# A hybrid decoder layer: x and first weights interleaved, three column tiles on each quarter of x, later bias table, swapped attention outputs

## The chip, the cores and the metric

The kernel runs on one core of a Trainium2 chip. Its time is the device time of one execution in microseconds (us); before the change the median of three runs is 1372.5 us (1372.31 to 1373.0). Lower is better. The engines are TensorE (PE: matmuls, with PEld its weight loads), VectorE (DVE), ScalarE (ACT), GpSimd (POOL) and SyncE (SP, which here only issues DMAs).

## The reference

One layer of a causal decoder trunk for 256 tokens of 2048 features, all in fp32. Three sub-layers follow each other, each normalised before and after and added to the residual stream:

- a token mixer: `z = rmsnorm(x) @ w_in`, whose columns feed 12 heads of dilated window attention (64 wide, with a relative-position bias from a 32-row table), 512 channels of chunked spatial gating, and 12 heads of RWKV-7 (a recurrent state with data-dependent decay); their outputs go through `w_out`;
- cross-attention, 4 heads over 256 memory tokens;
- a gated MLP with 5632 hidden features and a causal convolution of width 3 (its taps) on the up-projection.

The attention part, cut to what matters here (one of three window patterns):

```python
scores = einsum(q, k) * dh ** -0.5
scores = where(valid, scores + bias, NEG_INF)
p = exp(scores - max(scores))
o = einsum(p, v) / sum(p)
```

The kernel merges the three patterns into one: the bias of a distance has the logarithm of the number of patterns that hold it added, and impossible distances get -1e30. The 12 head outputs together are then normalised (rmsnorm over 768 columns).

## The kernel before

**Products in split precision.** Each weight tile is loaded in pieces of 512 KB (`raw_load`, L217, on SP's queue, four buffers), and `split` (L227) makes two parts of it: a high part by a rounding copy on ACT (L233) and a low part, the rest, by a subtraction on DVE (L235); three buffers each. Activations have high and low parts too. A product then is three matmuls: high x high (L265), high x low (L267), low x high (L270), into a PSUM tile `mm`. `wstat` (L254) keeps weights stationary and streams 256 tokens; `xstat` (L291) keeps activations stationary and streams 512 columns (L306, L308, L312). A unit of 1024 weight elements per partition is split and used at once.

**Opening.** The pool `sp` takes x in eight tiles (two token halves of four column quarters), issued on SP (L416), with the first low-rank weights behind the first quarter. A table of gains, `grow` (64 rows, in two loads from ACT's queue, L433 and L434), is transposed on TensorE into `gpar` (L448, L449). `transposed` (L362) transposes x, two 128-column blocks at a time (L371), scales by the gain and splits into hT (ACT L357, DVE L358). `row_factors` (L384) squares and sums x on ACT (L391), and a power on POOL (L396) gives the row factor; `over_rows` (L399) spreads it (L403). Then come small parameters (`prow`, nine loads on SP, L486, transposed at L491), the bias table (`tab`, `oneh`, `lnc`: one small matmul, L510, an addition, L511, a store `toep` to DRAM, L513) and the convolution taps (`crow`, four transposes, L522, into `cw`).

**Main products and lanes.** The mixer's main stream of products runs over column tiles in a written order: the low-rank columns (128), three key tiles, three receptance and three value tiles of RWKV (256 columns each, L977), the gate's low-rank columns, attention's values, then q, k pairs and the gating columns (L1217 to L1224), then `w_out`. Beside it run lanes: generators for decays, keys, the triangular inverse, values, state, and later attention and gating (both only after the state is done). `Lanes` (L120) keeps its own clock, a planner's estimate: after each unit of main products it moves on by 2.6 us per eight blocks, and a lane that yielded a number of us is continued when that has passed; what a lane then puts on TensorE is placed behind the last main product. `L.drain` (L162) runs lanes until a condition holds. Then a scheduler of the language orders each engine's instructions by priority and its own estimate of when they are ready; `issue_after` pins an order on one engine only, and `high_priority` lifts instructions forward. Engines take their instructions in that fixed order.

**Parts of the lanes.** `decays` (L608) loads two small weights into one buffer `wa` from ACT's queue (L612, L613), multiplies them with the low-rank activations `zl` (L621), and takes sigmoids (L626) and later exponentials (L641, L642). `keys` (L661) squares (L669), sums (L674), takes a power on POOL (L680), spreads it (L682) and transposes it (L692).

**Attention.** `b12` (L1021) reads the stored table `toep` back from DRAM as 128 shifted rows for 12 heads, 1.5 MB. For each of three groups of four heads, two heads at a time: scores (L1038), addition of the bias and maxima on DVE (L1043 to L1047), exponentials on ACT with their sums (L1049, L1051), three transposes of the weights per head (L1059), and the outputs with the weights stationary and the values (64 columns) moving (L1066, L1068, L1070): tokens lie on the partitions. The result is divided by the sums (L1076), squared and summed (L1080); at the end it is scaled by the row factor (L1090), transposed (L1097) and split with a gain.

## Time and profile before

| | before |
|---|---|
| median of 3 runs | 1372.5 us |
| profiled execution, its own time | 1375.61 us |
| its span | 1373.9 us |
| mean granted TensorE clock | 0.993 |
| TensorE busy | 1337.0 us (97%) |
| VectorE / ScalarE / GpSimd busy | 869.4 / 715.7 / 149.6 us |

The profile is of one execution, recorded by the hardware; its span leaves out a little at either end. Rows of instruction groups give line, engine, operation, output <- inputs, shape, count, then busy time and the mean duration of one in ns, then the idle time of the engine before them and what ended it. A matmul's end is modelled, so that its duration is longer than its place in the stream: what one costs in a row of equals is the distance between starts, or the time per instruction in the chain of waits. fp32 matmuls count as two instructions each, those of split parts as one. In rows in order of time the first number is the start in us from the span's start, the second the time until the last of the group has ended; what stands in brackets is idle time of the engine before it and what ended that. Rows of waits give total us, times, and the longest.

### The profile page before, as it was taken

The page shows a single profiled execution, that of the slowest core. Times are in us where ns is not written, and L with a number is a line of the kernel's source. Part 1 is how long each engine was busy: PE and PEld are TensorE (multiplying, and loading weights), DVE is VectorE, ACT ScalarE, POOL GpSimd, SP SyncE. Part 2 cuts the span into 40 slices and gives each one's busy share as a digit, 9 for nine tenths or more (in the row PEclk, how much of TensorE's full clock was granted, in tenths as well). Part 3 has the DMA queues.
Part 4 walks back from the last instruction along what each step waited for, and adds up shares of the span by engine and source line. Part 5 has one row for each costly group of instructions (what it writes and reads, how often), then busy time and mean ns, then how long its engine had stood idle before and what let it go on. Part 6 is the DMA issues. An engine that isn't in the chain of part 4 may idle for free.

```text
span 1373.9 us, 20692 instructions
## 1 busy us (share of the span) xinstructions
PE 1337.0 (97%) x8036; PEld 1175.1 (86%) x8036; DVE 869.4 (63%) x1277; ACT 715.7 (52%) x1097; POOL 149.6 (11%) x185
## 2 busy tenths in 40 slices
PE   6899999999999999999999999999999999999997
PEld 6889989999987879878888888888888888888886
DVE  5579964456555766567767676767676674444444
ACT  5755363244446656456555555555555553434442
POOL 3011100120003110001111111111111120000001
PEclk9999999999999999999999999999999999999999
DMA  7545553145547755444655656666666666556663
GB/s 219 157 137 156 146 173 94 55 148 149 147 142 258 255 181 166 157 148 132 190 185 184 185 186 189 188 188 184 184 186 187 188 218 194 193 195 191 195 196 128
DMA packets 189840, 238.80 MB, mean 174 GB/s; under 512 B 7920, under 2 KB 144013, under 8 KB 189741
## 3 DMA queue, kind: packets, MB, share of 16 engines
q1 hardware_dynamic: 185802, 225.76, 53.1%
q0 software_dynamic: 3376, 11.29, 2.5%
q8 instruction: 63, 1.03, 0.3%
q10 hardware_dynamic: 563, 0.43, 0.1%
q14 instruction: 36, 0.29, 0.1%
HBM read 235.33 MB, written 2.12 MB: 173 GB/s over the span
## 4 chain that ended last, share of the span: by engine, by line
PE 91%; issue 3%; DVE 2%; DMA 1%; ACT 1%; POOL 1%; ACTq 0%; DVEq 0%; POOLq 0%
PE mm L284 24%; PE mm L286 12%; PE mm L306 10%; PE mm L308 10%; PE mm L312 10%; PE mm L265 6%; PE mm L270 5%; PE mm L267 5%; PE auxq L657 1%; DMA wa<-in_rwkv_w_up_dram 1%; DVE lo L235 1%; PE auxq L774 1%; PE auxp L774 1%; DMA raw<-in_w_in_dram 0%; ACT hi L233 0%
## 5 line engine op out<-in xcount | busy, mean ns | idle before, releaser
L235 DVE TENSOR_TENSOR lo<-raw,hi 128x1024 fp32r<-128x1024 f32 x422 | 517.5, 1227 | 392.9 <-ACT hi L233 391.6
L233 ACT CAST hi<-raw 128x1024 fp32r<-128x1024 f32 x422 | 442.9, 1050 | 468.0 <-PE mm L308 171.6
L284 PE MATMUL mm<-h,hi 128*128 128x512 f32 x1376 | 486.3, 399 | 0.0
L286 PE MATMUL mm<-h,lo 128*128 128x256 f32 x1376 | 386.5, 281 | 0.0
L284 PEld LDWEIGHTS mm<-h,hi 128*128 128x128 f32 x1376 | 258.6, 188 | 64.4
L286 PEld LDWEIGHTS mm<-h,lo 128*128 128x128 f32 x1376 | 260.0, 189 | 0.0
L265 PE MATMUL mm<-h,hi 128*128 128x256 f32 x624 | 162.6, 293 | 2.0 <-ACT h L357 2.0
L267 PE MATMUL mm<-h,hi 128*128 128x256 f32 x624 | 160.2, 288 | 0.7 <-DVE h L358 0.7
L308 PE MATMUL mm<-hi,hid 128*128 128x512 f32 x352 | 136.9, 389 | 0.0
L306 PE MATMUL mm<-hi,hid 128*128 128x512 f32 x352 | 136.9, 389 | 0.0
L265 PEld LDWEIGHTS mm<-h,hi 128*128 128x128 f32 x624 | 120.8, 195 | 4.3 <-ACT h L357 2.2
L267 PEld LDWEIGHTS mm<-h,hi 128*128 128x128 f32 x624 | 120.6, 194 | 1.7 <-DVE h L358 1.0
L1419 POOL TENSOR_TENSOR z<-z,rrow 128x256 f32<-128x256 f32 x86 | 70.7, 822 | 427.5 <-DVE z L1418 427.5
L312 PE MATMUL mm<-lo,hid 128*128 128x512 f32 x352 | 108.4, 389 | 0.0
L270 PE MATMUL mm<-h,lo 128*128 128x256 f32 x624 | 102.5, 286 | 0.0
L270 PEld LDWEIGHTS mm<-h,lo 128*128 128x128 f32 x624 | 87.2, 193 | 1.3 <-issue 1.0
L306 PE MATMUL mm<-hi,h 128*128 128x512 f32 (+1 forms) x208 | 79.1, 385 | 1.4 <-ACT hi L233 1.4
L312 PEld LDWEIGHTS mm<-lo,hid 128*128 128x128 f32 x352 | 66.1, 188 | 13.8
L308 PEld LDWEIGHTS mm<-hi,hid 128*128 128x128 f32 x352 | 66.1, 188 | 13.7
L306 PEld LDWEIGHTS mm<-hi,hid 128*128 128x128 f32 x352 | 66.0, 188 | 13.7
L308 PE MATMUL mm<-hi,h 128*128 128x512 f32 (+1 forms) x208 | 77.0, 375 | 0.0
L312 PE MATMUL mm<-lo,h 128*128 128x512 f32 (+1 forms) x208 | 59.8, 375 | 0.2 <-DVE lo L235 0.2
(336 smaller groups left out, 1520.5 us busy)
## 6 DMA issues: line engine op xcount, KB each, us to landing
raw<-in_ffn_w_up_dram SPq DMA_DIRECT2D x176, 512.0 KB, 3.6
raw<-in_w_in_dram SPq DMA_DIRECT2D x94, 512.0 KB, 4.3
raw<-in_ffn_w_down_dram SPq DMA_DIRECT2D x88, 512.0 KB, 4.6
raw<-in_w_out_dram SPq DMA_DIRECT2D x32, 512.0 KB, 5.0
raw<-in_mem_wkv_dram SPq DMA_DIRECT2D x16, 512.0 KB, 4.1
raw<-in_mem_wq_dram SPq DMA_DIRECT2D x8, 512.0 KB, 3.8
raw<-in_mem_wo_dram SPq DMA_DIRECT2D x8, 512.0 KB, 3.7
x<-in_x_dram SPq DMA_DIRECT2D x8, 256.0 KB, 7.4
```

The lines of the kernel that those rows point to most:

```text
L233: nc.scalar.copy(hv, rv)
L235: nc.vector.tensor_tensor(lv, rv, hv.bitcast(F32), op=ALU.subtract)
L265: nc.tensor.matmul(o, lhsT=hv[:, k, cs], rhs=X.h(k0 + k), start=(k0 + k == 0), stop=False)
L267: nc.tensor.matmul(o, lhsT=hv[:, k, cs], rhs=X.l(k0 + k), start=False, stop=False)
L270: L.last = nc.tensor.matmul(o, lhsT=lv[:, k, cs], rhs=X.h(k0 + k), start=False, stop=(k0 + k == nk - 1))
L284: nc.tensor.matmul(view(ps[t], z=2, t=S), lhsT=hv[:, k, cs], rhs=X.hl[k0 + k], start=(k0 + k == 0), stop=False)
L286: L.last = nc.tensor.matmul(ps[t][:, S:], lhsT=lv[:, k, cs], rhs=X.h(k0 + k), start=False, stop=(k0 + k == KT - 1))
L306: nc.tensor.matmul(o, lhsT=X.h(kk)[:, ts_], rhs=hv[:, k, :], start=(first and k0 + k == 0), stop=False)
L308: nc.tensor.matmul(o, lhsT=X.l(kk)[:, ts_], rhs=hv[:, k, :], start=False, stop=False)
L312: L.last = nc.tensor.matmul(o, lhsT=X.h(kk)[:, ts_], rhs=lv[:, k, :], start=False, stop=(last and k0 + k == nk - 1))
L774: nc.tensor.matmul(pv[:, n, c0:], lhsT=BN[:, g * 4 + n, :], rhs=G[g][:, n, c0:], start=True, stop=True)
L1419: nc.gpsimd.tensor_tensor(z, z, x2row, op=ALU.mult)
```

## The change

- **Opening.** SP issues x by quarters, with the low-rank weights (for quarters 0 and 2) and a quarter of the first key tiles' weights between them. Per quarter, `prepare` transposes and splits x and splits the weights, and three column tiles (low-rank, and two of the first key tile) take their products from it; the order on SP, ACT, DVE and TensorE is pinned by `queued`. The square sums of a quarter follow its splits on ACT. The first two `wstat` calls are gone.
- **Small loads.** `grow` has 48 rows; the memory gain's 16 rows (`grow2`), the nine parameter loads and the six decay weights (now three buffers, all loaded ahead) are issued from POOL.
- **Bias table and taps** move from the opening into the attention lane, with their loads on POOL and buffers of attention.
- **Lanes.** `keys` yields 5.5 in place of 3.5; the decays' exponentials are pinned behind the last sigmoid on ACT.
- **Attention.** The weights are divided by their sums before the transposes; the outputs have the values (64 columns) stationary and 256 or 128 tokens moving, so that they come out transposed, two heads on the two halves of the partitions. Squares are added over heads on POOL, summed over partitions by a small matmul, the row factor is spread by another, and the last transposes are gone.
- **Sizes.** Small tiles have 8 columns in place of 16; `v` and `oc` have rows of 544 in place of 516; two unused fillers are added.

```diff
+        cp.tile([P, 64], F32, name="fill")
...
-            return mk(cp, tag, bufs, (P, 16))[:, :n]
+            return mk(cp, tag, bufs, (P, 8))[:, :n]
...
+        def queued(*engines):
+            with_ = ExitStack()
+            for e in engines:
+                if e in last:
+                    with_.enter_context(tc.issue_after(last[e].ins))
+            return with_
...
+            nc.scalar.dma_start(grow, gains[0:6:2].rearrange("g (k p) -> g k p", p=P))
+            xt = [[], []]
+            raws = {}
+            for c in range(4):
+                with queued("SP"):
+                    load_row(xt, x2d, c, lambda: mk(sp, "x", 8), nc.sync)
+                if c % 2 == 0:
+                    with queued("SP"):
+                        raws["LO", c] = raw_load(w_in, 4 * c, 8, COL_LO, P, 0)
+                with queued("SP"):
+                    raws["K", c] = raw_load(w_in, 4 * c, 4, COL_CK, 2 * P, 0)
...
+            def prepare(c):
+
+                nonlocal lo_w, k_w
+                with queued("ACT", "DVE", "PE"):
+                    for _ in transposed(hT, xt, gcol(0), hbuf, js=(2 * c, 2 * c + 1), banks=(auxp, auxp)):
+                        pass
+                if c % 2 == 0:
+                    with queued("ACT", "DVE"):
+                        lo_w = split(raws["LO", c], 8, P, 0)
+                with queued("ACT", "DVE"):
+                    k_w = split(raws["K", c], 4, 2 * P, 0)
+
+            def first_products(c, o, w, k0, cs):
+                for k in range(4 * c, 4 * c + 4):
+                    for n, (wk, xk) in enumerate(((w[0], hT.h(k)), (w[0], hT.l(k)), (w[1], hT.h(k)))):
+                        L.last = last["PE"] = nc.tensor.matmul(o[:, :S], lhsT=wk[:, k - k0, cs], rhs=xk,
+                                                               start=(k == 0 and n == 0),
+                                                               stop=(k == KT - 1 and n == 2))
...
+            prepare(0)
+            for c in range(4):
+                kw = k_w
+                first_products(c, ps_lo, lo_w, 8 * (c // 2), slice(0, P))
+                first_products(c, ps_k[0], kw, 4 * c, slice(0, P))
+                if c < 3:
+                    prepare(c + 1)
+                    with queued("ACT"):
+                        square_sums(part, xt, c + 1, lambda: mk(sp, "tmp", 4))
+                first_products(c, ps_k[1], kw, 4 * c, slice(P, 2 * P))
+        rx = row_factors(xt, None, part)
...
-            nc.sync.dma_start(prow[r0:r0 + n, :], src.rearrange("(n p) -> n p", p=P))
+            nc.gpsimd.dma_start(prow[r0:r0 + n, :], src.rearrange("(n p) -> n p", p=P))
...
-            return mk(mp, "v", 3, (P, 516))
+            return mk(mp, "v", 3, (P, 544))[:, :516]
...
-            for i in range(3):
-                wa = mk(rp, "wa", 1, (P, 256))
-                nc.scalar.dma_start(wa[0:64, :], a["rwkv_w_up"][0][:, i * 256:(i + 1) * 256])
-                nc.scalar.dma_start(wa[64:128, :], a["rwkv_a_up"][0][:, i * 256:(i + 1) * 256])
+            was = [s1() for _ in range(3)]
+            for i, wa in enumerate(was):
+                nc.gpsimd.dma_start(wa[0:64, :], a["rwkv_w_up"][0][:, i * 256:(i + 1) * 256])
+                nc.gpsimd.dma_start(wa[64:128, :], a["rwkv_a_up"][0][:, i * 256:(i + 1) * 256])
...
+                with tc.issue_after(sig.ins):
+                    nc.scalar.activation(E2, E, AF.Exp, scale=KAPPA)
+                    nc.scalar.activation(E, E, AF.Exp, scale=-KAPPA)
...
-            yield 3.5
+            yield 5.5
...
+            rows, taps = et(), et()
+            nc.gpsimd.dma_start(rows[:REL_BUCKETS, :A_HEADS], a["rel_bias_table"])
+            nc.gpsimd.dma_start(rows[:REL_BUCKETS, P:P + 384], a["c_onehot"])
+            lnc = et()[:A_HEADS, :384]
+            nc.gpsimd.dma_start(lnc, a["c_lncount"])
...
+            yield 4.0
+            ps = auxp()
+            nc.tensor.matmul(ps[:A_HEADS, :384], lhsT=rows[:REL_BUCKETS, :A_HEADS], rhs=rows[:REL_BUCKETS, P:P + 384],
+                             start=True, stop=True)
+            nc.vector.tensor_tensor(lnc, ps[:A_HEADS, :384], lnc, op=ALU.add)
+            nc.gpsimd.dma_start(toep, lnc)
...
+                    nc.vector.reciprocal(rden, den)
+                    for e, sc in enumerate(scs):
+                        for b, w in ((0, slice(0, 128)), (1, slice(128, 384))):
+                            nc.vector.tensor_scalar(sc[:, w], sc[:, w], rden[:, 2 * e + b:2 * e + b + 1],
+                                                    None, op0=ALU.mult)
...
+                    for b, w in ((0, slice(0, S)), (1, slice(P, S))):
+                        for e in range(2):
+                            nc.tensor.matmul(po[64 * e:64 * e + 64, c0 + w.start:c0 + w.stop],
+                                             lhsT=vhead(b, 4 * j + e0 + e),
+                                             rhs=pts[e][:, b * S:b * S + w.stop - w.start],
+                                             start=(b == 0), stop=(b == 1))
...
+            for b in range(2):
+                nc.tensor.matmul(ps[:, b:b + 1], lhsT=asq[:, b * P:(b + 1) * P], rhs=cmask[:, 1, P - 1:P],
+                                 start=True, stop=True)
...
+                nc.tensor.matmul(ps[:, b * P:(b + 1) * P], lhsT=ars[:, b:b + 1].to_broadcast([P, P]), rhs=ident,
+                                 start=True, stop=True)
...
+            res.tile([P, 120], F32, name="fill2")
```

More of the change, by code (lines that the diff above doesn't have):

```diff
@@ L231, in split @@
             lv = lo[:, :nk * nco].rearrange("p (k c) -> p k c", k=nk)
-            with tc.high_priority(offset=AHEAD):
-                nc.scalar.copy(hv, rv)
-                with tc.issue_after(gcopy.ins):
-                    nc.vector.tensor_tensor(lv, rv, hv.bitcast(F32), op=ALU.subtract)
+            with tc.high_priority(offset=ahead):
+                last["ACT"] = nc.scalar.copy(hv, rv)
+                last["DVE"] = nc.vector.tensor_tensor(lv, rv, hv.bitcast(F32), op=ALU.subtract)
             return hv, lv
@@ new lines, in hybrid_block @@
+            nc.vector.memset(mhalf, -0.5)
+            nc.scalar.activation(small(1), mhalf[:, :1], AF.Square)
+            make_identity(nc, ident)
+            part = mk(cp, "rpart", 2, (P, 8))
+            ps_lo = auxq()
+            ps_k = [mmps(), mmps()]
+            lo_w = k_w = None
+            def prepare(c):
[8 more added lines that the diff above has]
+                    k_w = split(raws["K", c], 4, 2 * P, 0)
@@ new lines, in hybrid_block @@
+            ps = auxp()
+            nc.tensor.transpose(ps[:, :3 * KT], grow, ident[:3 * KT, :3 * KT])
+            last["DVE"] = nc.vector.tensor_copy(gpar[:, :3 * KT], ps[:, :3 * KT])
+            prepare(0)
+            for c in range(4):
+                kw = k_w
[6 more added lines that the diff above has]
+                first_products(c, ps_k[1], kw, 4 * c, slice(P, 2 * P))
@@ L981, in hybrid_block @@
                 g = new()
-                ps = wstat(w_in, col + i * 256, 2 * P, hT)
+                ps = [p[:, :S] for p in ps_k] if (key, i) == ("K", 0) else wstat(w_in, col + i * 256, 2 * P, hT)
                 gv = view(g, k=2, t=S)
```

198 lines of the change are left out of this document (82 added, 116 removed).

## The prediction

> **What bounds the kernel now.** I read the page first, then the engines by stretches of the opening, then what TensorE waited for, then the opening in order of time.
>
> ```profile
> PE 1337.0 (97%) x8036; PEld 1175.1 (86%) x8036; DVE 869.4 (63%) x1277; ACT 715.7 (52%) x1097; POOL 149.6 (11%) x185
> PE 91%; issue 3%; DVE 2%; DMA 1%; ACT 1%; POOL 1%; ACTq 0%; DVEq 0%; POOLq 0%
> ```
>
> TensorE is the bound: 97% busy, 91% of the chain that ends last. So a change can save only TensorE's idle time and TensorE's own work.
>
> ```profile
> core 0: us, PE busy (x) PEld busy (x) DVE busy (x) ACT busy (x) POOL busy (x), PEclk, DMA share, GB/s
> 0.00:10.00 10.00, 1.30 (x6) 1.21 (x7) 1.25 (x7) 4.23 (x8) 1.49 (x9) 1.00 0.69 204
> 10.00:20.00 10.00, 6.86 (x45) 6.22 (x44) 6.60 (x13) 7.37 (x18) 0.00 (x0) 1.00 0.95 283
> 20.00:30.00 10.00, 10.00 (x74) 10.00 (x73) 6.87 (x13) 6.95 (x16) 4.94 (x3) 0.83 0.57 164
> 30.00:40.00 10.00, 8.11 (x64) 7.29 (x63) 5.76 (x7) 2.09 (x2) 4.75 (x5) 1.00 0.84 256
> 300.00:420.00 120.00, 120.00 (x815) 107.66 (x814) 76.11 (x140) 60.73 (x114) 3.93 (x6) 1.00 0.50 148
> ```
>
> Of the 37 us in which TensorE is idle, 14 lie in the first 40. In the attention's stretch (300 to 420) it has none, so there only its own work counts.
>
> ```profile
> PE auxp L448 <- DMA grow<-in_mem_src_gain_dram: 8.7, 1, 8.7
> PE mm L265 <- ACT h L357: 2.0, 1, 2.0
> PE auxp L510 <- issue: 1.9, 1, 1.9
> PE auxp L692 <- ACT et L682: 1.6, 1, 1.6
> PE auxp L621 <- DMA wa<-in_rwkv_w_up_dram: 1.3, 1, 1.3
> ```
>
> These waits are what the change touches: the last part of the gain table, the opening's order, the bias table (L510), a decay weight (L621) and the keys' factor (L692).
>
> ```profile
> L265 PE MATMUL mm<-h,hi x48: 278/283/562, 12.3 to 39.6; 128*128 128x256 f32 x48
> L267 PE MATMUL mm<-h,hi x48: 278/283/519, 13.4 to 39.7; 128*128 128x256 f32 x48
> L270 PE MATMUL mm<-h,lo x48: 280/283/416, 20.2 to 40.2; 128*128 128x256 f32 x48
> ```
>
> This is my yardstick: the products of the low-rank tile and of the first key tiles are 144, and the last starts at 40.2 us. After it TensorE is nearly full, so whatever brings number 144 forward reaches the end.
>
> **The opening.** The same 5 MB (x 2, low-rank weights 1, key weights 2) are loaded by SP, now in quarters, and three column tiles use each quarter of x at once. By 20 us the rates above (204 and 283 GB/s over 10 us each) have moved 4.9 MB, so data is no longer late where the order asks for it at the pace worked out below.
>
> ```profile
> 6.75 0.63 ACT L391 ACTIVATE tmp<-x 128x512 f32<-128x512 f32 x1 [1.78 <-DMA x<-in_x_dram]
> 8.70 1.05 ACT L233 CAST hi<-raw 128x1024 fp32r<-128x1024 f32 x1 [1.22 <-DMA raw<-in_w_in_dram]
> 9.78 1.23 DVE L235 TENSOR_TENSOR lo<-raw,hi 128x1024 fp32r<-128x1024 f32 x1 [0.47 <-ACT hi L233]
> 11.89 0.84 ACT L357 ACTIVATE h<-auxp,gpar 128x256 fp32r<-128x256 f32 x2 [0.19 <-DVE h L358]
> 12.99 0.67 PE L371 MATMUL auxp<-ident,x 128*128 128x128 f32 x4
> 16.64 1.04 ACT L233 CAST hi<-raw 128x1024 fp32r<-128x1024 f32 x1 [2.44 <-DMA raw<-in_w_in_dram]
> 22.11 0.41 PE L267 MATMUL mm<-h,hi 128*128 128x256 f32 x1
> 22.32 0.41 PE L265 MATMUL mm<-h,hi 128*128 128x256 f32 x1
> ```
> ```profile
> 29.84 0.48 PE mm L270 x4
> 320.40 0.66 PE auxp L1059 x6
> ```
>
> A product takes 0.12 us, a 128-column transpose 0.11. Per quarter, counted from its first transpose: four transposes and the hop, 0.75 (as in the opening rows); four copies on ACT at 0.42, to 2.4; the key weights' high part 1.05, to 3.4; their low part on DVE 1.23, to 4.65. Meanwhile TensorE does the last quarter's twelve products and the low-rank tile's twelve (hidden); from 4.65 it does eleven key products, to 5.9, and only then come the next transposes. Quarter 2 also splits low-rank weights: ACT 1.05 more, DVE's two subtractions end at 3.45 + 2 x 1.23 = 5.9, next quarter at 7.2. Quarter 0: x is there at 6.75, with two square sums ahead on ACT; low-rank weights at 8.7; the key weights next in SP's queue some 1.7 later (512 KB at 300 GB/s), low part at 12.6, first key products done by 14 to 16, since the early products run at 0.21 (rows at 22). From 15: 5.9 + 7.2 + 5.9 + the last twelve 1.44 gives 35.5; I take 36. Ends: 33 (nothing cold, the splits overlap better) and 41 (cold throughout). The gain is 4.2, less TensorE work that was already done by 40.2 and now comes later, the bias table's:
>
> ```profile
> 37.60 0.80 PE L510 MATMUL auxp<-oneh,tab 32*12 32x384 f32 x2 [1.89 <-issue]
> 25.06 0.71 POOL L396 TENSOR_TENSOR rs<-small,mhalf 128x2 f32<-128x2 f32 x1 [22.93 <-DVE small L395]
> 39.87 0.55 POOL L513 DMA_DIRECT2D toep<-lnc  x1 [5.25 <-DVE lnc L511]
> ```
>
> **3.4 us** remain (ends 6.4 and -1.6). The L510 wait of 1.9 is inside this. The square sums move between the splits on ACT: 4.3 to 5.3 us of ACT work in quarters of 5.9 to 7.2, hidden. Sixteen small loads (parameters, mem gain, six decay weights) leave SP's and ACT's queues for POOL's: 16 x 0.55 = 9 us, in the 22.9 us in which POOL only waits. If they were issued behind the two big memsets after that power instead, they would come some 5 us late, and the decays with them.
>
> **Lanes.** The decay weights get three buffers: 1.3 us. The keys' transposes are issued 2 later in the planner's time, so the 1.6 us wait for L682 goes. The zl chain gets less cover, since its first products come straight behind the opening: I give back 0.7. Net **2.2 us** (ends 0.5 and 3.5). Sigmoids before exponentials save table loads,
>
> ```profile
> 47.42 1.28 ACT L626 ACT_TABLE_LOAD   x1
> ```
>
> two or three of them at 1.28; ACT is not the bound there, so nothing. The lanes start one key tile later against the main products (96 x 0.12 = 11.5 us less cover); attention's later groups wait for the main k tiles anyway, so nothing, at worst -3.
>
> **Attention.** Before, each pair of heads takes twelve 64-column instructions:
>
> ```profile
> 313.41 0.33 PE L1066 MATMUL auxq<-v,et 128*128 128x64 f32 x2
> ...
> 314.79 0.71 PE L1038 MATMUL auxp<-col,col 64*128 64x128 f32 x6
> ```
> ```profile
> 267.00 0.43 PE auxp L953 x2
> 304.59 0.86 PE auxp L1038 x8
> ```
>
> So 1.38 per pair, 8.3 for six pairs, and twelve transposes (L1097) at 0.11 = 1.3. Swapped, a pair has four instructions of 256 columns and four of 128, two heads on different halves of the output partitions, and no transposes at the end. One by one that is 4 x 0.215 + 4 x 0.11 = 1.30, 7.8 in all; L1038, the same eight sizes on two halves of the rows, takes 0.86, 5.2 in all. Added: four small matmuls, eight instructions at 0.11, 0.9. The saving is 0.9 to 3.5; I take **3.0**, nearer to L1038, since it is the same shape.
>
> [...]
>
> DVE gains 24 scalings and loses six and three broadcasts:
>
> ```profile
> L1090 DVE TENSOR_SCALAR ca<-ca,small 128x256 f32<-128x256 f32 x6 | 1.7, 348 | 0.8 <-POOL small L327 0.8
> ```
>
> At most 24 x 0.35 = 8 us more in 120 us where DVE is busy for 76: hidden; without that cover TensorE would wait for the low parts.
>
> The bias table now follows the state stage: loads, product, addition, a store to DRAM, the wide load.
>
> ```profile
> toep<-lnc POOLq DMA_DIRECT2D x1, 18.0 KB, 2.0
> ze<-toep POOLq DMA_DIRECT2D x1, 1536.0 KB, 9.7
> 300.81 0.64 POOL L1115 TENSOR_SCALAR_AFFINE_SELECT nat<-nat 128x512 f32<-128x512 f32 x1 [7.01 <-DMA nat<-in_sgu_w_dram]
> ```
>
> From the product to the landed bias: 0.8 + 0.55 + 2.0 + 9.7 = 13 us, against 3 of lane time before the scores; the first bias additions wait on DVE with splits queued behind them. The planner may hold these back, and splits run up to three tiles ahead, so I give back **1 us** (ends 0 and 13).
>
> **Aligned tiles and fillers.** The profile shows no addresses. Nearest are the products that read oc, one of the resized tiles, beside those that don't:
>
> ```profile
> L306 PE MATMUL mm<-hi,h 128*128 128x512 f32 x66 | 26.8, 406 | 0.0
> L306 PE MATMUL mm<-hi,oc 128*128 128x512 f32 x24 | 9.9, 411 | 0.0
> ```
>
> A difference of 5 ns on 72 products is 0.4 us either way; I take zero.
>
> **Sum.** 3.4 + 2.2 + 3.0 - 1.0 = 7.6 us. The profiled execution took 1375.6 (span 1373.9), 3.1 above the median of 1372.5; the saving is taken off the median: **1365 us**.
>
> **Rivals.**
> 1. The opening gives nothing: the copy, split and subtraction of each quarter keep number 144 near 40. For it: the 5.9 to 7.2 us a quarter are nearly all ACT and DVE, with TensorE behind them. Against: before, ACT's second split also waited 2.4 us for its weights (row at 16.64), with transposes' copies queued behind it. 1372.5 - 4.2 = 1368.3.
> 2. The clock. Before, TensorE was busy for 6.9 of the 10 us from 10 on, and the next 10 were granted 0.83, with products at 0.21. If the new order's pauses do this twice, some 36 more products and transposes on the path pay 0.1 each: 3.6 us, and 1369. [...]
> 3. Slower: the bias arrives late. The store waits in POOL's queue behind a mask that waits up to 7.0 us for its own load (row at 300.81), and the wide load after it; DVE stops at the addition. 13 + 7 - 3 of lane time = 17, less about 4 covered by tiles already split, is 13 us on TensorE: 1372.5 - 8.6 + 13 = 1377. It decides once the bias lands more than some 13 us after its scores. Against: the planner orders by its own reckoning of DMAs and may put main work ahead.
> 4. The order does nothing for time because planner shifts elsewhere cost as much: 1372.5.
>
> **How the numbers follow.** Chances: forecast 0.55 (its own range 1361 to 1369), rival 1 0.13, rival 2 0.10, rival 3 0.13, rival 4 0.09. A measurement of this kernel tells about 0.2%, 2.7 us. Faster: forecast, rival 1 and most of rival 2, 0.75; same: 0.12; slower: 0.13. The range leaves out rival 3 and the best corner of all terms (6.4 + 3.5 + 3.5 would be 1359): 1358 to 1373.
>
> **What will show it.** Number 144 starts at 33 to 38; the L510 and L621 waits are gone and L692's is under 0.5; quarters of 6 to 7 us in the opening; the swapped pairs take about 0.86 each; no gap on TensorE near the first score additions. Wrong if: PEclk falls in the second or third window; DVE waits for the ze load for more than 5 us; a swapped pair takes 1.3.

## The result and the profile after

The changed kernel takes 1379.7 us (median of 1376.7 to 1382.3), beside 1372.4 us for the kernel before on the same chip: ratio 1.0047, 95% interval 1.0029 to 1.0065. It is **slower**, by 6.5 us by the ratio and 7.3 by the medians, where I forecast 7.6 us less. Its profiled execution took 1379.5 us, close to its median.

The page of the changed kernel, busy time and the shares of the chain that ended last:

```profile
PE 1339.2 (97%) x8009; PEld 1169.8 (85%) x8009; DVE 876.3 (64%) x1302; ACT 708.0 (51%) x1083; POOL 166.3 (12%) x212
PE 89%; issue 4%; DVE 3%; ACT 2%; DMA 1%; POOL 1%; DVEq 0%; SPq 0%; POOLq 0%; ACTq 0%
```

TensorE is still the bound, with 27 instructions fewer but 2 us more of busy time, and the chain now runs through other engines for two points more. The stretches that I showed of before, now of the changed kernel (busy us and instructions of each engine, granted clock, DMA share, GB/s):

```profile
10.00:20.00 10.00, 9.20 (x54) 8.82 (x55) 4.38 (x7) 4.21 (x8) 3.53 (x7) 1.00 1.10 317
20.00:30.00 10.00, 7.80 (x62) 7.19 (x61) 5.43 (x7) 6.26 (x15) 0.00 (x0) 1.00 0.41 116
30.00:40.00 10.00, 9.58 (x78) 9.13 (x78) 7.41 (x12) 6.92 (x12) 4.72 (x3) 1.00 0.55 172
300.00:420.00 120.00, 117.43 (x776) 100.37 (x775) 80.74 (x174) 54.64 (x110) 13.38 (x17) 0.99 0.47 143
```

The opening is better filled. (Its clock of 1.00 from 10 to 20 us is measured only from 16.5 us on, where the records of the clock begin; until then products start 0.21 us apart, and 0.12 after.) The attention's stretch, which had no idle time at all before, has 2.6 us now and a clock below 1. What TensorE waited for in the changed kernel (total, times, longest):

```profile
PE auxp L493 <- DMA grow<-in_sandwich_gains_dram: 5.5, 1, 5.5
PE auxq L487 <- ACT hi L240: 3.9, 2, 2.5
...
PE auxp L1113 <- DVE et L1107: 2.0, 1, 2.0
PE auxp L651 <- ACT oc L656: 1.8, 1, 1.8
...
PE mm L318 <- DVE lo L241: 1.3, 1, 1.3
...
PE mm L312 <- ACT hi L240: 1.0, 1, 1.0
```

L493 and L487 are the opening. The other four are new or larger: the transposes of the probabilities (L1113) wait for DVE's scalings, the decays' second step (L651) for the sigmoids of the first, and the first tile of attention's values (L312, L318) for its splits. The waits at L510, L621 and L692 are gone.

The 6832 products of the main stream are the same in both kernels, so they can be counted off and compared. From the starts in the traces, the time (us) at which each part's last product begins:

| part | before | changed | table in a lane (e6) | lanes later (e9) | swap and table lane (e17) |
|---|---|---|---|---|---|
| low-rank and first key tile (144) | 40.2 | 37.3 | 36.4 | 41.8 | 38.9 |
| third key tile | 69.9 | 68.6 | 70.5 | 71.6 | 71.9 |
| second low-rank tile | 171.9 | 167.4 | 169.6 | 171.6 | 170.1 |
| first values tile (512 wide) | 195.0 | 192.8 | 195.3 | 198.5 | 193.1 |
| gate Bg | 327.5 | 318.1 | 319.7 | 325.3 | 322.3 |
| gate Bu | 411.0 | 414.3 | 407.7 | 414.6 | 406.2 |
| end of the span | 1373.9 | 1377.8 | 1370.4 | 1377.8 | 1368.2 |

From the gate Bu on all kernels run alike, within some 2 us. The changed kernel's lead of some 3 us at product 144 is 1.3 two tiles later; the 9.4 at Bg are not a saving, since lane work that lay ahead of Bg now lies behind it; by Bu the lane work is done in both and the changed kernel is some 3 us behind. (Before's profiled execution was 3 us over its median, so the median says 7.) The loss is made between product 144 and Bu. What of it lies behind Bg is best seen against e6, whose lane work lies in the same places: from Bg to Bu the changed kernel takes 96.2 us, e6 88.0. Of these 8.2 us TensorE's idle time is 2.2 (e6 has none), the half clock shown below costs 1.7 by estimate (half of its 3.4 us), and the table's product and the taps, which e6 has elsewhere, take about 1; some 3 us, in which TensorE is busy, are not accounted for. The same holds from product 144 to Bu against before: 377.0 us beside 370.8, with 8.2 us idle beside 5.5.

The chain that ended last, in the changed kernel (start, us, step):

```profile
319.87 0.76 PE auxp L1060 x2
...
320.65 0.56 DVE et L1062
...
321.49 2.96 DMA toep<-et
...
325.02 9.86 DMA ze<-toep
...
334.90 0.29 DVE et L1091
...
340.14 0.30 DVE et L1107
...
340.49 0.33 PE auxp L1113
```

From the table's product to the landed bias it is 15 us. The first scores were issued at 324.3; their additions begin at 334.9, the scalings at 340.1, and TensorE stops before the first transpose. What followed, in windows of the changed kernel of 3.4 us, the step in which the records of the clock change (the columns as above):

```profile
337.30:340.70 3.40, 1.35 (x12) 1.15 (x10) 3.37 (x8) 3.15 (x8) 0.00 (x0) 1.00 0.14 14
340.70:344.10 3.40, 3.40 (x19) 2.92 (x18) 2.70 (x5) 0.00 (x0) 0.00 (x0) 0.50 0.88 292
```

TensorE was busy for 1.35 of 3.4 us, and the next 3.4 us ran at half clock. The clock isn't what sets the two kernels apart, though: ahead of Bu the profiled execution of before has two such half-clock windows (at 19.9 and 262.3 us), the changed one only this. Over all executions the mean granted clock is 0.9935 in the four of the changed kernel and 0.9933 in the 17 of before in group 1.

### The profile page after: what moved, and what is told of

The parts are those of the page before. It is cut to its first block, busy times and chain, and to the rows that moved or that the text cites. A ratio compares the mean times of both kernels' runs of the same rounds, so it can differ in the third digit from the quotient of the medians.

```text
span 1377.8 us, 20669 instructions
## 1 busy us (share of the span) xinstructions
PE 1339.2 (97%) x8009; PEld 1169.8 (85%) x8009; DVE 876.3 (64%) x1302; ACT 708.0 (51%) x1083; POOL 166.3 (12%) x212
## 4 chain that ended last, share of the span: by engine, by line
PE 89%; issue 4%; DVE 3%; ACT 2%; DMA 1%; POOL 1%; DVEq 0%; SPq 0%; POOLq 0%; ACTq 0%
PE mm L290 23%; PE mm L292 12%; PE mm L312 10%; PE mm L314 10%; PE mm L318 10%; PE mm L271 5%; PE mm L276 5%; PE mm L273 5%; DVE lo L241 1%; PE mm L487 1%; PE auxq L688 1%; DMA ze<-toep 1%; ACT hi L240 1%; PE auxp L805 1%; PE auxq L805 1%
## 5 line engine op out<-in xcount | busy, mean ns | idle before, releaser
L241 DVE TENSOR_TENSOR lo<-raw,hi 128x1024 fp32r<-128x1024 f32 x422 | 516.8, 1226 | 388.7 <-ACT hi L240 386.8
L292 PE MATMUL mm<-h,lo 128*128 128x256 f32 x1376 | 386.5, 281 | 0.0
L290 PEld LDWEIGHTS mm<-h,hi 128*128 128x128 f32 x1376 | 258.6, 188 | 64.4
L292 PEld LDWEIGHTS mm<-h,lo 128*128 128x128 f32 x1376 | 260.0, 189 | 0.0
L271 PE MATMUL mm<-h,hi 128*128 128x256 f32 x576 | 148.2, 291 | 0.0
L273 PE MATMUL mm<-h,hi 128*128 128x256 f32 x576 | 146.7, 286 | 1.1 <-DVE h L364 1.1
L312 PE MATMUL mm<-hi,hid 128*128 128x512 f32 x352 | 136.9, 389 | 0.0
L273 PEld LDWEIGHTS mm<-h,hi 128*128 128x128 f32 x576 | 111.2, 193 | 2.5 <-DVE h L364 1.3
L271 PEld LDWEIGHTS mm<-h,hi 128*128 128x128 f32 x576 | 110.5, 193 | 2.9 <-issue 1.3
L318 PE MATMUL mm<-lo,hid 128*128 128x512 f32 x352 | 108.4, 389 | 0.0
L276 PE MATMUL mm<-h,lo 128*128 128x256 f32 x576 | 95.8, 286 | 0.0
L276 PEld LDWEIGHTS mm<-h,lo 128*128 128x128 f32 x576 | 81.0, 193 | 0.4 <-issue 0.3
L312 PE MATMUL mm<-hi,h 128*128 128x512 f32 (+1 forms) x208 | 79.2, 386 | 1.0 <-ACT hi L240 1.0
L318 PEld LDWEIGHTS mm<-lo,hid 128*128 128x128 f32 x352 | 66.1, 188 | 13.8
L312 PEld LDWEIGHTS mm<-hi,hid 128*128 128x128 f32 x352 | 66.1, 188 | 13.7
L318 PE MATMUL mm<-lo,h 128*128 128x512 f32 (+1 forms) x208 | 60.8, 378 | 1.4 <-DVE lo L241 1.3
```

The lines of the kernel that those rows point to most:

```text
L241: last["DVE"] = nc.vector.tensor_tensor(lv, rv, hv.bitcast(F32), op=ALU.subtract)
L271: nc.tensor.matmul(o, lhsT=hv[:, k, cs], rhs=X.h(k0 + k), start=(k0 + k == 0), stop=False)
L273: nc.tensor.matmul(o, lhsT=hv[:, k, cs], rhs=X.l(k0 + k), start=False, stop=False)
L276: L.last = nc.tensor.matmul(o, lhsT=lv[:, k, cs], rhs=X.h(k0 + k), start=False, stop=(k0 + k == nk - 1))
L290: nc.tensor.matmul(view(ps[t], z=2, t=S), lhsT=hv[:, k, cs], rhs=X.hl[k0 + k], start=(k0 + k == 0), stop=False)
L292: L.last = nc.tensor.matmul(ps[t][:, S:], lhsT=lv[:, k, cs], rhs=X.h(k0 + k), start=False, stop=(k0 + k == KT - 1))
```

## The experiments

The kernels below ran beside the kernel before on the same chip, whose median there is in the third column. All times in us.

| run | median | before | ratio | 95% interval |
|---|---|---|---|---|
| changed kernel | 1379.7 | 1372.4 | 1.0047 | 1.0029 to 1.0065 |
| e1 changed, table in the opening | 1376.0 | 1374.5 | 1.0007 | 0.9997 to 1.0018 |
| e2 changed, outputs not swapped | 1379.8 | 1374.5 | 1.0042 | 1.0030 to 1.0054 |
| e3 changed, old opening | 1381.1 | 1374.5 | 1.0051 | 1.0038 to 1.0064 |
| e4 changed, table in the opening, not swapped | 1379.0 | 1374.5 | 1.0043 | 1.0028 to 1.0057 |
| e5 before + new opening | 1381.2 | 1375.1 | 1.0050 | 1.0036 to 1.0065 |
| e6 changed, table in a lane of its own | 1373.2 | 1375.1 | 0.9990 | 0.9981 to 0.9999 |
| e7 changed, lanes' edits undone | 1384.0 | 1375.1 | 1.0072 | 1.0058 to 1.0086 |
| e8 changed, old tile sizes | 1380.7 | 1375.1 | 1.0041 | 1.0029 to 1.0053 |
| e9 before, lanes added one tile later | 1377.4 | 1374.2 | 1.0025 | 1.0013 to 1.0037 |
| e10 e6 + longer time between decays | 1375.8 | 1374.2 | 1.0009 | 0.9999 to 1.0019 |
| e11 e6 + time ahead of the inverse's copies | 1376.1 | 1374.2 | 1.0017 | 1.0007 to 1.0026 |
| e12 e6 + both | 1375.3 | 1374.2 | 1.0011 | 1.0000 to 1.0023 |
| e13 before + swap | 1372.1 | 1374.0 | 0.9989 | 0.9977 to 1.0001 |
| e14 before + lanes' edits | 1379.5 | 1374.0 | 1.0044 | 1.0029 to 1.0060 |
| e15 before + late table | 1379.1 | 1374.0 | 1.0033 | 1.0020 to 1.0047 |
| e16 before + swap and lanes' edits | 1374.8 | 1374.0 | 1.0009 | 0.9996 to 1.0021 |
| e17 before + swap and table lane | 1368.5 | 1374.9 | 0.9948 | 0.9929 to 0.9967 |
| e18 e17 + three decay weights | 1372.4 | 1374.9 | 0.9981 | 0.9968 to 0.9995 |

Differences between two rows carry both intervals, so they are good to some 2 to 2.5 us.

### Group 1: undo one part

e1 puts the table and the taps back into the opening:

```diff
+        nc.tensor.matmul(ps[:A_HEADS, :384], lhsT=tab, rhs=oneh, start=True, stop=True)
...
-            rows, taps = et(), et()
...
-            nc.vector.tensor_copy(cw, ps[:, :4 * NF].rearrange("p (j n) -> p j n", j=4))
             b12 = view(mk(rp, "ze", 1, (P, 3072)), h=A_HEADS, x=256)
```

> The changed kernel with the bias table and the taps loaded and multiplied in the opening again, as before the change; all else as changed. Theory A (the late bias is the loss): in the changed kernel's trace the first score addition waits 3.3 us for the wide load, the probabilities' transposes 2.05 us for their scalings, and the clock falls for 3.4 us behind that; 300 to 430 us holds 9.2 us more idle time on TensorE than before the change. Without the late bias most of it goes: 1379.7 - 7 + 2 (the opening gets the table's product and its loads back) = 1375, at most 1376.5, and no wait for the wide load. Theory B (the swapped outputs and their scalings are the loss): unchanged within 2 us, 1378 to 1381, and the transposes still wait. Theory C (the new opening bunches the lane work): also 1378 to 1381.

Ratio 1.0007: 5.5 us less than the changed kernel, as theory A has it. (The 9.2 us of added idle time from which I argued was misread: TensorE is busy for 126.4 of the 130 us from 300 on, and for all of them before, so it is 3.6.) But its opening pays: in its second key tile TensorE waits twice, first for `zl` and then for the sigmoids, the second time as in the changed kernel.

```profile
PE auxp L670 <- ACT oc L675: 1.8, 1, 1.8
PE auxp L670 <- ACT zl L1020: 1.3, 1, 1.3
```

e2 takes back the swapped outputs and keeps the late table:

```diff
-                                             lhsT=vhead(b, 4 * j + e0 + e),
-                                             rhs=pts[e][:, b * S:b * S + w.stop - w.start],
...
+                        nc.tensor.matmul(ov[:, 0, e, :], lhsT=pT[:, 0:P], rhs=vhead(0, h),
+                                         start=True, stop=True)
```

> The changed kernel with the attention outputs computed as before the change (probabilities stationary, the division after, twelve transposes at the end); the bias table stays late. Theory A (late bias): the first addition still waits some 3 us, and TensorE loses the 1.6 us that the swap saves in its own work: 1380 to 1382. Theory B (the 24 scalings on DVE ahead of the transposes, and the tiling changes, cost more than the swap saves): 1379.7 - 4 = 1376 or lower, and TensorE's wait for the transposes' input falls from 2.05 to under 1. Theory C (opening): 1379 to 1382.

No difference (1.0042). Theory B falls as far as it says that the scalings and the tilings cost more than the swap saves; theory A's loss of the swap's saving doesn't show either.

e3 is the kernel before with everything but the opening:

```diff
-            for c in range(4):
-                kw = k_w
-                first_products(c, ps_lo, lo_w, 8 * (c // 2), slice(0, P))
...
+        ps = wstat(w_in, COL_LO, P, hT)
```

> The kernel before with every part of the change but the opening: late bias, swapped outputs, aligned tiles, three decay weights, later keys. Theory A or B: the loss in the attention stays and the 3 us that the opening gained are gone: 1381 to 1384. Theory C (the opening's third column tile moves the lanes one key tile later and bunches their work): the loss goes with it, 1370 to 1374, and the groups of attention lie as before the change.

1.0051: beside the rest of the change, the opening is worth nothing that can be measured. Theory C, as the whole cause, falls.

e4 joins e1 and e2, so the attention is that of before:

```diff
-            rows, taps = et(), et()
...
-                                             lhsT=vhead(b, 4 * j + e0 + e),
```

> The changed kernel with both the bias table and the attention outputs as before the change: the new opening, the three decay weights, later keys and aligned tiles alone. By my sum of terms for these, 1372.4 - 3.4 - 2.2 + 1 (the table's product back in the opening) = 1368. Theory A or B: 1366 to 1371, since nothing of the changed attention is left. Theory C: 1377 to 1381, still slower than before the change.

1.0043, 1379.0 us, where theories A and B expected 1366 to 1371 and theory C, which fell in e3, 1377 to 1381. So a second loss stands in the opening and the lanes. And e4 against e1 prices the swap with the table early: 4.9 us.

### Group 2: the table's place, the opening alone, lanes, tiles

e5 is the kernel before with the new opening alone, the same edit as e3 the other way round:

```diff
+                first_products(c, ps_lo, lo_w, 8 * (c // 2), slice(0, P))
+                first_products(c, ps_k[0], kw, 4 * c, slice(0, P))
...
-        ps = wstat(w_in, COL_LO, P, hT)
```

> The kernel before with the new opening alone (loads interleaved, three column tiles on each quarter, small loads on POOL's queue); lanes, tile sizes, bias table and attention are those of before. Theory D (the low-rank tile is now done at the same time as the key tile, so the decays' chain behind it has less to hide under, and a halved clock follows the stall): what the opening wins by product 144 (1.3 to 3.8 us in the runs so far) is lost again before the second key tile is done, and the kernel is slower than before by 2 to 5 us, ratio 1.0015 to 1.0035. My first reckoning: faster by 3.4 us, ratio 0.9975. If the loss of 4.5 us in the run with both halves of the attention as before is due to the lanes' edits: ratio below 1.000.

1.0050: 6 to 7 us slower, over the 2 to 5 that theory D has. TensorE's waits between 40 and 210 us in e5:

```profile
PE mm L317 <- DVE lo L240: 3.2, 1, 3.2
PE auxp L668 <- DMA wa<-in_rwkv_w_up_dram: 2.4, 1, 2.4
PE auxp L668 <- ACT zl L1017: 1.3, 1, 1.3
```

The rows of the kernel before for the same three:

```profile
PE auxp L621 <- DMA wa<-in_rwkv_w_up_dram: 1.3, 1, 1.3
PE mm L306 <- ACT hi L233: 0.6, 1, 0.6
...
PE auxp L621 <- ACT zl L971: 0.3, 1, 0.3
```

e6 leaves the wide load behind the state stage and moves only the table's loads, product and store, and the taps, into a lane that starts with the others:

```diff
+        def tables():
+            w = mk(rp, "ze", 1, (P, 3072))
...
+            yield 16.0
+            ps = auxq()
+            nc.tensor.matmul(ps[:A_HEADS, :384], lhsT=tab, rhs=oneh, start=True, stop=True)
+            nc.vector.tensor_tensor(lnc, ps[:A_HEADS, :384], lnc, op=ALU.add)
+            nc.gpsimd.dma_start(toep, lnc)
...
+        L.add(tables())
```

> The changed kernel with the bias table's product, its store and the taps' transposes put into a lane of their own that starts in the second key tile, in the buffer that the wide bias load uses later; the wide load alone stays behind the state stage. Theory A (late bias): the first addition waits for no load and TensorE not for the scalings, as with the table in the opening, while the second key tile keeps the cost it has in the changed kernel (2.4 us more than before, not 8): 1376.0 - 5 = 1371, faster than before by some 3 us, ratio 0.997 to 0.999. If the lateness is the wide load's alone: as the changed kernel, ratio 1.004 to 1.006.

0.9990: this one move is worth 0.0057, 7.8 us (against e8 in the same group, the changed kernel but for its tile sizes, 7.0 us). The wide load, in the changed kernel and in e6 (POOL's instructions in order of time):

```profile
325.02 1.07 POOL L1070 DMA_DIRECT2D ze<-toep  x1 [2.33 <-DMA toep<-et]
```
```profile
305.53 1.09 POOL L1073 DMA_DIRECT2D ze<-toep  x1 [0.50 <-PE auxp L955]
```

It goes out 19.5 us earlier; its 9.0 us are hidden, and what TensorE waits for between 300 and 430 us in e6 is one row:

```profile
PE auxq L1230 <- DVE et L1221: 1.0, 1, 1.0
```

The changed kernel has this wait too (L1227, 1.0), and the 2.0 at L1113 beside it.

e7 undoes the lanes' edits in the changed kernel:

```diff
-                with tc.issue_after(sig.ins):
...
-            yield 5.5
+            yield 3.5
```

> The changed kernel with the lanes' edits undone: one buffer for the decay weights and their loads on ACT's queue, sigmoids and exponentials in the planner's own order, the keys' transposes two units earlier. My term for these was a gain of 2.2 us (1.3 for the weights, 1.6 for the transposes, less 0.7): undone, the kernel should be 2 us slower than the changed one, ratio 1.006. If the sigmoids' pin makes the decays' third step wait (1.8 us in the changed kernel): the same or faster by 1 to 2 us, ratio 1.003 to 1.005, and the wait of TensorE for the decays' sigmoids goes while the waits for the weights and the keys' factor come back.

1.0072: in the changed kernel these edits are worth 3.4 us, near my term of 2.2 and not far over what such a difference is good to.

e8 takes back the tile sizes:

```diff
-            return mk(mp, "oc", 6, (P, 544))[:, :516]
+            return mk(mp, "oc", 6, (P, 516))
```

> The changed kernel with the tile sizes of before: 516 columns for v and oc, 16 for the small ones, no fillers. I took this part at nothing, plus or minus 0.4 us: the ratio stays at 1.004 to 1.006 and the products that read oc take the same time.

1.0041: nothing, as forecast.

### Group 3: is it the place of the lanes?

e9 is the kernel before with the lanes, and the shift and tanh that make their `zl`, placed one key tile later, and nothing else:

```diff
-        L.add(chain(decays(), *(keys(i) for i in range(3)), inverse()))
...
                 ps = wstat(w_in, col + i * 256, 2 * P, hT)
+                if (key, i) == ("K", 0):
...
+                    L.add(chain(decays(), *(keys(i) for i in range(3)), inverse()))
```

> The kernel before, with one thing moved: the low-rank tile's shift and tanh and the adding of the lanes come behind the products of the first key tile instead of ahead of them; loads, opening, attention unchanged. Theory D (what costs the new opening its gain is that a key tile's 11.5 us no longer cover the decays' chain and that all lane work lies a tile later): slower than before by 3 to 7 us, ratio 1.002 to 1.005, with waits of TensorE for the decays in the second key tile and more waiting around the first values tile (2 to 3 us against 1.1). If the new opening's loads, splits or clock are the cause: ratio 0.999 to 1.001.

1.0025, 3.4 us slower, with no other part of the change in it. That is half of e5's loss; of the rest, e5's rows show the weights' wait 1.1 us longer than before and the wait for `zl` 1.0 us longer, and the remainder is open. Its longest wait after the opening's own is e5's, to the digit:

```profile
PE mm L312 <- DVE lo L235: 3.2, 1, 3.2
```

and the window of the stall and the one after it, in e9:

```profile
181.30:184.70 3.40, 0.39 (x2) 0.35 (x3) 3.40 (x3) 1.51 (x1) 0.00 (x0) 1.00 0.00 0
184.70:188.20 3.50, 3.50 (x10) 2.72 (x9) 2.30 (x3) 3.46 (x4) 0.00 (x0) 0.51 0.75 203
```

DVE is busy for the whole of the first. In the changed kernel's order of time the same work stands there:

```profile
180.67 2.07 DVE L777 STREAM_TRANSPOSE k<-k 128x1024 f32<-128x1024 f32 x1
182.66 1.18 DVE L241 TENSOR_TENSOR lo<-raw,hi 128x1024 fp32r<-128x1024 f32 x1
183.88 1.73 DVE L743 COPY ze<-k 32x768 f32<-32x768 f32 x2
185.94 1.25 DVE L783 STREAM_TRANSPOSE k<-k 128x1024 f32<-128x1024 f32 x1 [0.34 <-ACT ze L745]
```

It is the end of the inverse: long instructions with the next weights' splits (L241) queued between them. Before the change the same transposition began ten us earlier, in the second low-rank tile, and TensorE waited 0.6 in the values tile (row above):

```profile
170.87 2.08 DVE L746 STREAM_TRANSPOSE k<-k 128x1024 f32<-128x1024 f32 x1
```

e10 to e12 try to mend e6 by the planner's times: between the decays' steps, ahead of the inverse's copies, and both.

```diff
-                yield 2.0
+                yield 4.0
...
             nc.vector.transpose(view(Tz, n=32, m=32), t3.rearrange("p n m -> p m n"))
+            yield 3.0
```

> The kernel with the table in a lane of its own, and the planner's time between the decays' three steps 4.0 instead of 2.0, so that each step's weights are issued when the sigmoids of the step before have freed its two banks. Theory D: the wait of 1.8 us for the decays' sigmoids goes, and the halved clock of 3.4 us behind it (1.1 us of loss): 1373.2 - 2.5 = 1370.7, ratio 0.997. If the stall is only pushed on (the keys wait in its place): 1373, ratio 0.999.

> The kernel with the table in a lane of its own, and 3.0 of planner time between the inverse's transposition on DVE and the four copies that read it, so that ACT's two copies are not issued some 5 us before their input is there with the splits of the next weights queued behind them. If that queueing is what makes TensorE wait 1.3 + 1.0 us in the first values tile: ratio 0.9975, about 2 us less, and that wait goes. If DVE's own load (transposition 2.1, copies, second transposition 1.25) makes it: no change, ratio 0.999.

> The table in a lane of its own with both of the planner's times changed (4.0 between the decays' steps, 3.0 ahead of the inverse's copies). If both single edits act and are independent: 1373.2 - 2.5 - 2 = 1368.7, ratio 0.9955. If the lanes only shift their stalls: 0.998 to 1.000.

1.0009, 1.0017, 1.0011, against e6's 0.9990 in another group: no gain from any, and e11 is 3.7 us slower. In e10 the decays' wait falls from 1.8 to 1.0 and a new one of 1.8 comes later:

```profile
PE auxq L858 <- DVE v L617: 1.8, 1, 1.8
PE mm L312 <- ACT hi L240: 1.1, 1, 1.1
PE auxp L651 <- ACT oc L656: 1.0, 1, 1.0
```

In e11 ACT's copies wait for the transposition for 5.1 us as they do in e6, and the waits of 1.3 and 1.1 in the first values tile stay. So the edit never reached ACT's order, and whether that queueing or DVE's own load makes the stall is open. In e12 the stall in the values tile is down to 0.2, and waits of 1.8 and 1.4 stand elsewhere in the lanes: they shift their stalls.

### Group 4: one part alone

e13, e14 and e15 add the swap, the lanes' edits, or the late table to the kernel before (the diffs of e2, e7 with the three weights, and e1, the other way round); e16 the first two. From e14's edit:

```diff
+            was = [s1() for _ in range(3)]
...
+                nc.gpsimd.dma_start(wa[0:64, :], a["rwkv_w_up"][0][:, i * 256:(i + 1) * 256])
```

> The kernel before with the swapped attention outputs alone. My term: 3.0 us less (0.9 to 3.5), ratio 0.998. With the table in the opening the swap was worth 4.9 us beside the new opening (1.0043 to 1.0007): by that 0.9965. With the late table it was worth nothing (1.0042 to 1.0047). [...]

> The kernel before with the lanes' edits alone: three buffers for the decay weights, loaded by POOL's queue; exponentials pinned behind the last sigmoid; the keys' transposes two units later. My term: 2.2 us less (0.5 to 3.5), ratio 0.9984; undoing them in the changed kernel cost 3.4 us, which gives 0.9975. If their worth hangs on the new opening: 0.999 to 1.001.

> The kernel before with the bias table and the taps moved behind the state stage, alone. My term: 1 us slower beside 1.9 us that the opening gets back: ratio 0.9985 to 1.0005. Theory A as the runs have it so far (1.0047 late against 0.999 early, with the swapped outputs): slower by 5 to 8 us less the opening's 2, ratio 1.002 to 1.005. If the late table hurts only where the lanes already lie a key tile later: 0.999 to 1.001.

> The kernel before with the swapped outputs and the lanes' edits, and neither the new opening nor the late table. If those two were the losses and the other two add up by my terms (3.0 + 2.2): ratio 0.9962; by the runs so far (4.9 + 3.4): 0.994. Then it beats the kernel before, the changed kernel and the one with the table in a lane of its own (0.999). If the gains of the two hang on the new opening: 0.998 to 1.000.

The swap alone gives 1.5 us, and its interval just takes in no difference. The late table alone costs 4.5 us. Not all of that need be the late bias: DVE waits 3.1 us for the wide load and TensorE 1.6 for the exponentials, but TensorE also waits 2.1 us for the keys' factor (1.6 before). The lanes' edits alone, a gain of 3.4 in the changed kernel, cost 6 us here. With the swap added to them (e16) 1.2 us of loss are left, inside the interval: beside them the swap is worth 4.8, not 1.5. The waits of e14 between 40 and 210 us:

```profile
PE mm L312 <- DVE lo L235: 2.9, 1, 2.9
PE auxp L622 <- ACT oc L627: 1.8, 1, 1.8
PE auxq L807 <- DVE et L801: 0.9, 1, 0.9
```

The same stall again in the first values tile: three keys of two units each push the inverse later, as the missing tile did in e9 (its transposition starts at 181.8 us, in e9 at 181.3, before at 170.9). e16 has the same stalls of 2.9 and 1.8 us, so they alone don't set the time. The 1.8 is the changed kernel's wait for the sigmoids, which came with the weights' wait of 1.3 removed.

### Group 5: leave the lanes where they were

e17 is the kernel before with the swap and e6's table lane; opening, lanes' times and tiles are untouched. e18 adds the three early weights.

```diff
+        L.add(tables())
...
+                                             lhsT=vhead(b, 4 * j + e0 + e),
...
```

> The kernel before with the swapped outputs, and with the bias table and taps in a lane of their own in the second key tile (loads in the opening, the wide load where it was). Opening, lanes' times and tile sizes as before the change. The opening loses the table's product and its wait (1.9 to 2.2 us) and the lanes stay where they were. If the swap's 1.5 us and these 2 add up: ratio 0.9970 to 0.9980, faster than all kernels so far. If the shift of the lanes by the table's own instructions is enough to bring a new stall: 0.999 to 1.002.

> The same, and the three buffers of the decay weights loaded early by POOL's queue, without the exponentials' pin and without the later keys. If the wait of 1.3 us for the second weight is simply saved: 1.3 us less than the kernel without it, ratio about 0.9965. If the decays then stall on their sigmoids, as in the lanes' edits alone (1.8 us, 1.0044): 1.000 to 1.003.

e17: 1368.5 us, ratio 0.9948 (0.9929 to 0.9967): 7 us **faster than before**, the fastest of all, and 3 us better than the sum that I expected. Its waits between 40 and 210 us:

```profile
PE auxp L603 <- DMA wa<-in_rwkv_a_up_dram: 1.4, 1, 1.4
PE mm L306 <- ACT hi L233: 0.6, 1, 0.6
PE auxp L674 <- ACT et L664: 0.5, 1, 0.5
```

The first values tile has before's 0.6 again. Against e13 the table lane is worth 5.6 us: the product's wait in the opening (2.2 in e13) is gone and nothing waits for the bias later. e18 (0.9981, between my two cases) removes the 1.4 and is 4.5 us slower than e17; in its place stand the two waits below, which don't make up 4.5 us:

```profile
PE auxp L675 <- ACT et L665: 1.6, 1, 1.6
...
PE auxp L604 <- ACT oc L609: 1.2, 1, 1.2
```

## Why the prediction was wrong, step by step

| step | forecast | alone in before | in the changed kernel |
|---|---|---|---|
| opening | -3.4 | +6.9 (e5) | -0.5 (e3) |
| lanes | -2.2 | +6.0 (e14) | -3.4 (e7) |
| attention, swap | -3.0 | -1.5 (e13) | +0.7 (e2); -4.9 beside an early table (e4, e1) |
| late table | +1.0 | +4.5 (e15) | +7.8 against a lane (e6), +5.5 against the opening (e1) |
| tiles | 0 | not run | +0.8 (e8) |

(us, from the ratios times 1374; minus is faster.)

**What bounds the kernel** was read rightly: only TensorE's idle time and own work count.

**The opening's own sum was right, its worth was not.** I had product 144 at 36 us; it starts at 37.3. I had the quarters at 5.9, 7.2 and 5.9 after a first that ends near 15. Their transposes, in the changed kernel:

```profile
5.77 2.36 PE L376 MATMUL auxp<-ident,x 128*128 128x128 f32 x8
16.58 1.04 PE L376 MATMUL auxp<-ident,x 128*128 128x128 f32 x8
22.70 1.03 PE L376 MATMUL auxp<-ident,x 128*128 128x128 f32 x8
30.06 1.03 PE L376 MATMUL auxp<-ident,x 128*128 128x128 f32 x8
```

6.1 and 7.4 for the next two quarters, and 7.2 from the last transposes to number 144, where I had 5.9 and twelve products of 0.12, 7.3; only the first quarter, at 16.6 in place of 15, was off. What failed is the sentence that "whatever brings number 144 forward reaches the end". It holds only if the work behind 144 stays covered, and the edit that brought 144 forward took the cover away.

**The step that failed first: "The lanes start one key tile later ... so nothing, at worst -3".** I reasoned from the last groups of attention, which wait for the main tiles anyway. The loss is at the other end: at the decays, whose inputs are now late (zl), and at the inverse, which falls into the first values tile. e9 shows 3.4 us for this shift alone. The bound of 3 was nearly right; the value in the sum, nothing, was not. The 0.7 that I gave back for the zl chain was small too: with the new opening TensorE waits 1.3 for zl in e1 and e5, and 1.8 for the sigmoids behind it in e1 and the changed kernel.

**The step that failed most: "I give back 1 us (ends 0 and 13)" for the late table.** It costs 7.8 us against a lane, inside my bounds and far from my value. I counted 13 us from the product to the landed bias (it is 15) and named 3 us of lane time against it, then trusted the planner and three tiles of splits to cover the rest. The planner did put other work ahead: DVE waits only 3.3 us for the load, under the 5 that I had set as the sign of failure. But the whole chain of scores, additions, scalings and transposes started 10.6 us late, TensorE waited 2.0, and half a clock for 3.4 us followed, which I had not priced. These two come to 3.7 of the 7.8 us. Rival 3 had the place and the sign (1377 against 1379.7); its mechanism, a store waiting 7 us behind the mask on POOL, did not happen: the store went out ahead of the mask. That its time came so near is luck, since it priced the late bias at 13 us and let all other gains stand.

```profile
321.49 0.55 POOL L1063 DMA_DIRECT2D toep<-et  x1 [14.55 <-DVE et L1062]
322.05 0.65 POOL L1172 TENSOR_SCALAR_AFFINE_SELECT nat<-nat 128x512 f32<-128x512 f32 x1
```

**The lanes' edits**: the waits named did go (L621, L692), and the term is near what e7 measured. Alone they lose 6 us. That the sigmoids' place is worth nothing was not tested by itself. What the term missed is that with the weights there early TensorE waits for the sigmoids that free the decays' two banks: 1.8 us with the pin, 1.2 without it (e18).

**The swap** was priced well as TensorE's work. The changed kernel, at full clock and in full stretches:

```profile
380.62 0.87 PE L1121 MATMUL auxq<-et,v 128*64 128x256 f32 x8
```

0.87 for the eight of a pair, as L1038. Its worth of 4.9 beside an early table is over my end of 3.5, alone it is 1.5, and beside the late table nothing. That there the transposes wait for the bias's chain whatever TensorE saves is argued, not shown: e2, without the swap and its scalings, still loses the same time.

**Rival 2, the clock**, did not come true where I put it: from 16.5 us on the changed kernel's opening has the full clock. What came was a halved clock in the attention, where I had not looked for one: behind a stall of 2.0 us, 3.4 us ran at 0.50 (see the last section). Rival 1 (1368.3) and rival 4 (1372.5) both have the opening's gain lost or paid back, which is what the runs show, but put no loss beyond it. None of my three signs of being wrong came; of the signs of being right, one failed: TensorE does have a gap near the first score additions. (One quarter took 7.4 us where I had said 6 to 7.)

So the sum failed because its terms were added. Alone they come to +16 us, by the forecast to -7.6, and together to +6.5: each part moves the lanes against the main products, and pays or earns in the stalls and half-clock windows that this makes. That these account for all of the difference was not shown, and the idle time in the traces covers less than half of it; that the table's place and the lanes' place are the two largest causes, e6, e9 and e17 show.

## What to carry over

When an edit speeds up the work at the head of an engine's fixed order, ask first what that work was covering, and re-price what starts behind it: here a 3 us gain cost a tile of cover. A chain that ends in a wide transfer is costed from its first input to the last reader, and belongs well ahead of that reader, under work that covers it: the changed kernel with the same product in the opening, in an early lane and behind the state stage gave 1.0007, 0.9990 and 1.0047. And price edits together, or one at a time on a chip, when they share a schedule: the best kernel here (0.9948) keeps the swap, puts the table somewhere else and leaves the rest as it was.

## What the hardware showed that I had not expected

I had looked for a halved clock in the opening alone, and the changed kernel has one behind a short stall far from it. There a stall of 2.0 us left TensorE busy for 1.35 of 3.4 us, and the next 3.4 us ran at half clock. The two windows around its stalls of 1.3 and 1.0 us in the first values tile kept the full clock:

```profile
180.30:183.70 3.40, 2.30 (x11) 1.54 (x9) 3.33 (x4) 0.93 (x1) 0.00 (x0) 1.00 0.53 154
183.70:187.10 3.40, 2.18 (x9) 1.49 (x9) 3.02 (x4) 3.36 (x4) 0.00 (x0) 1.00 0.53 151
```

In the profiles of before and of the changed kernel every halving begins a whole multiple of 3.413 us after the first one (71, 176 and 395 times that in before, 83 and 302 in the changed kernel). I divided both profiles into such windows, from the first record of the clock on (13.1 and 16.5 us into the span). Of the windows at full clock the five in which TensorE was busy for 1.37 us or less were all followed by a halved one; of the twelve with 1.46 to 2.34 us one was, and of the 769 with 2.5 us or more one. So the profile's busy share doesn't settle it: the changed kernel's window of 1.46 us at 617.2 us kept the full clock behind it and its next one, of 1.67 us, did not, and the halved window of before at 262.3 us follows one in which TensorE was busy for 2.83 us. What halved the clock there is open. Executions of one kernel differ in time and in the clock granted: the twelve of e13 lie between 1369.3 us at 0.995 and 1375.7 at 0.991. What makes them differ was not shown.

The granted clock of each execution gives an estimate of what halved windows cost a kernel: its span times what the clock lacks to 1, on average, less the same of the kernel before beside it. By that, 5.0 of the 6.1 us that e14 loses on average are clock, 5.4 of 6.3 in e3, 2.8 of 6.9 in e5, 1.7 of 3.4 in e9 and 1.0 of 4.8 in e15, from 5 to 12 executions each. So by this estimate the lanes' edits alone cost mostly clock, the late table mostly not.
